# A decoder block's sub-norm: sum of squares from squared halves of the partitions, with one matmul of ones per head

## The chip, the cores and the metric

The kernel runs on one core of a Trainium2 chip. Its time is the device time of one execution in microseconds (us); the time of a kernel is the median over its runs. A core has five engines that run side by side, each through its own list of instructions in order: TensorE (PE in the profile, with its weight loads as PEld), VectorE (DVE), ScalarE (ACT), GpSimd (POOL) and SyncE (SP), which here only issues DMA transfers. GpSimd issues transfers too, those that add to what lies in SBUF.

## The reference, cut to what matters

One decoder block over 512 tokens of width 1024, all in float32:

```
h = rmsnorm(x, norm_attn_g);  q, k, v, u_pool, u_gate = split(h @ w_in)
for each of 8 heads:                          # two query/key pairs of width 64, one value of width 128
    w = softmax(q1 k1) - lam * softmax(q2 k2) # causal
    o = rmsnorm(w @ v, subln_g) * (1 - lam_init)     # the sub-norm: over the head's 128 value dims
x = x + (sigmoid(g_A) * o + sigmoid(g_P) * pool) @ w_out
x = x + square(relu(rmsnorm(x, norm_mlp_g) @ w_up)) @ w_down
return rmsnorm(x, final_norm_g)
```

The sub-norm divides each head's output, for each token, by the root of the mean of its 128 squares.

## The kernel before, in words

Everything lies in SBUF as 128 partitions by free columns. Activations are mostly kept transposed, features on the partitions and the 512 tokens along the columns; so a head's output o is a 128 x 512 tile whose 128 partitions are the value dims, and the sub-norm's sum runs over the partitions. For that, TensorE multiplies with a matrix of ones (`onesr`), which leaves the sum on every partition.

All matmuls run on float32 data split in two: a rounded high part (fp32r) and the rest as a low part, so a product of two matrices is three matmuls, high by high, low by high, high by low. In the names a leading `wh_`/`wl_` is the high and low part of a weight, `wr_` the raw weight as a transfer brings it. ScalarE's cast makes the high part (L112), VectorE's subtract the low one (L113). For squares the same is done: `sqh` is ScalarE's square rounded to fp32r, `sql` the rest, and `ss` is the sum of ones by `sqh` and ones by `sql`, two matmuls into one bank (L430, L431). GpSimd makes `sql` from o times o (L427) minus `sqh` (L428); for the last head VectorE does. `rsqrt` then makes y = 1/root from `ss`, on ScalarE (L202 to L204) and VectorE.

The stages in the profiled execution, by their time:

- 0 to 60 us: row norm, transposes, the value projection v.
- 60 to 305 us: the heads, one after another. `attn` makes the scores s (L395, L396), the softmax (L397 to L408, tile p), the transposes t (L410) and wt, then o (L418) and the sub-norm. Between the heads' matmuls stand the projections k, q, gate and pool of the next heads as fillers, so that TensorE has work while ScalarE and VectorE do softmax.
- 288 to 348 us: the out projection. po (L582 to L584) adds up `wh_o`/`wl_o` by vh/vl for four row tiles of 128 tokens and two column halves of 512: first the four tiles of the first half, then those of the second. When a tile's second half is done, VectorE adds it to x (L588, `x<-po`), ScalarE squares it with a sum over its row (L562), makes the root (L572 to L574), VectorE refines it (L575, L576) and scales the row (L637, `h<-x`); TensorE transposes h, four 128 x 128 pieces for each of two halves (L645, h2T), and ScalarE (L657) and VectorE (L658) split that into `gab`.
- 349 to 672 us: the MLP, in a scheme of Strassen's kind with sums of weight blocks. Products um (L782 to L788) from `gab` and from sums `gss` (L603, L604, by way of `hw`), z, then dm (L875 to L878). The sums of weights come about by transfers that GpSimd issues (L686, `wga_`, `wal_`) and that add to what lies in SBUF.

The order of each engine's instructions isn't written by hand. A scheduler lays them out when the kernel is built, with its own simulated timeline, over all five engines, from the data dependencies and the buffers of the tile pools (a tag with `bufs=2` has two buffers; the raw weights `wr_` have two, so a new transfer waits until the older one's cast and split have read it). Any edit can therefore change the order in places far from it.

Of the kernel before, what the change touches and what calls it, by code (L numbers as in the profile page):

```python
# [12 lines left out]
F32R = mybir.dt.float32r  # L13
I32 = mybir.dt.int32
AF = mybir.ActivationFunctionType
ALU = mybir.AluOpType
# [6 lines left out]
H = 8  # L23
# [28 lines left out]
def block_kernel(ctx, tc, xT, x_tok, gains, pos, consts, w_in, w_v, w_pool, w_out, w_up, w_dn, out):  # L52
    nc = tc.nc
    V, A, G, T = nc.vector, nc.scalar, nc.gpsimd, nc.tensor
# [32 lines left out]
    def tmp(tag, name, shape=(P, S), dt=F32, bufs=2):  # L87
        return tp.tile(list(shape), dt, tag=tag, name=name, bufs=bufs)

    def f(ap):  # L90
        return ap.bitcast(F32)
# [50 lines left out]
    for i in range(2):  # L142
# [14 lines left out]
    onesr = cp.tile([P, P], F32R, name="onesr")  # L157
# [7 lines left out]
        out=mask[:, 384:512], in_=mask[:, 384:512], pattern=[[-1, P]],  # L165
# [34 lines left out]
    def rsqrt(dst, src, t, n):  # L200

        A.activation(out=dst, in_=src, func=AF.Ln, scale=1.0 / n, bias=eps)  # L202
        A.activation(out=dst, in_=dst, func=AF.Exp, scale=-0.5)
        A.activation(out=t, in_=dst, func=AF.Square, scale=1.0 / math.sqrt(n))  # L204
        V.scalar_tensor_tensor(out=t, in0=src, scalar=n * EPS, in1=t, op0=ALU.add, op1=ALU.mult)
        V.scalar_tensor_tensor(out=dst, in0=t, scalar=-3.0, in1=dst, op0=ALU.add, op1=ALU.mult)
# [10 lines left out]
    for n in range(2):  # L217
# [43 lines left out]
        for t in range(NT):  # L261
# [4 lines left out]
                out=vd[2], in0=av, scalar=rcol[:, t, 0:1], in1=vd[1],  # L266
# [26 lines left out]
        out=r_, in0=posf.rearrange("p (t o) -> p t o", o=1).to_broadcast(sh),  # L293
        in1=invc.rearrange("p (o f) -> p o f", o=1).to_broadcast(sh), op=ALU.mult,
# [68 lines left out]
    lo_, hi_ = slice(0, 64), slice(64, 128)  # L363
# [22 lines left out]
    def attn(h, qs, ks, kz):  # L386
        wt = wt_all
        for i in range(NT):
            N = (i + 1) * P
            qsl = slice(i * P, i * P + P)  # L390
            pr = tmp(f"p{i}", f"p{h}_{i}", (P, 2, N), bufs=1)
            st = tmp("st", f"st{h}_{i}", (P, 6), bufs=3)
            for c in range(2):
                s_ = sbk(f"s{h}_{i}_{c}")
                T.matmul(s_[:, :N], lhsT=qs[:, c, qsl], rhs=ks[:, c, :N], start=True, stop=False)  # L395
                T.matmul(s_[:, :N], lhsT=qs[:, c, qsl], rhs=kz[:, c, :N], start=False, stop=True)  # L396
                V.tensor_tensor_reduce(  # L397
                    out=pr[:, c, :N], in0=s_[:, :N], in1=mask[:, S - N :], scale=-0.125, scalar=-NEG,
                    op0=ALU.add, op1=ALU.min, accum_out=st[:, c : c + 1],
                )  # L400
                A.activation(out=pr[:, c, :N], in_=pr[:, c, :N], func=AF.Exp, scale=-1.0,  # L401
                             bias=st[:, c : c + 1], accum_out=st[:, 2 + c : 3 + c])
            V.reciprocal(out=st[:, 4:6], in_=st[:, 2:4])
            V.tensor_scalar(out=st[:, 5:6], in0=st[:, 5:6], scalar1=lvec, scalar2=None, op0=ALU.mult)
            A.activation(out=pr[:, 1, :N], in_=pr[:, 1, :N], func=AF.Copy, scale=st[:, 5:6])
            V.scalar_tensor_tensor(out=pr[:, 0, :N], in0=pr[:, 0, :N], scalar=st[:, 4:5], in1=pr[:, 1, :N],
                                   op0=ALU.mult, op1=ALU.add)
            t_ = tbk(f"t{h}_{i}")  # L408
            for j in range(i + 1):
                T.transpose(out=t_[:, j * P : j * P + P], in_=pr[:, 0, j * P : j * P + P], identity=ident)  # L410
            tv = t_[:, :N].rearrange("p (j q) -> p j q", q=P)
            A.copy(out=wt[:, 0, : i + 1, qsl], in_=tv)
            V.tensor_tensor(out=wt[:, 1, : i + 1, qsl], in0=tv, in1=f(wt)[:, 0, : i + 1, qsl], op=ALU.subtract)
        o_ = obk(f"o{h}")
        n = 0
        for vv, ww in ((vh, 0), (vl, 0), (vh, 1)):
            for j in range(NT):
                T.matmul(o_[:, j * P :], lhsT=vv[:, h, j * P : j * P + P], rhs=wt[:, ww, j, j * P :], start=n == 0, stop=n == 11,  # L418
                         skip_group_check=True)
                n += 1  # L420
        o = tmp("o", f"o{h}", bufs=2)
        A.copy(out=o, in_=o_)
        sqh = tmp("sqh", f"sqh{h}", dt=F32R, bufs=1)
        A.activation(out=sqh, in_=o_, func=AF.Square)
        sql = tmp("y", f"sql{h}", dt=F32R, bufs=1)
        sq = tmp("sq", f"sqo{h}")
        (V if h == H - 1 else G).tensor_tensor(out=sq, in0=o, in1=o, op=ALU.mult)  # L427
        (V if h == H - 1 else G).tensor_tensor(out=sql, in0=sq, in1=f(sqh), op=ALU.subtract)  # L428
        ss = obk(f"ss{h}")
        T.matmul(ss, lhsT=onesr, rhs=sqh, start=True, stop=False)  # L430
        T.matmul(ss, lhsT=onesr, rhs=sql, start=False, stop=True)  # L431
        y = tmp("y", f"y{h}", bufs=1)
        rsqrt(y, ss, sq, P)
        if h == H - 1:
            return o, y
        V.scalar_tensor_tensor(out=o, in0=o, scalar=subc, in1=y, op0=ALU.mult, op1=ALU.mult)
        return o, None
# [78 lines left out]
    for h in range(H):  # L516
        outs[h] = attn(h, *cur)
        cur = qk(h + 1) if h < H - 1 else None
        while nf < LAG[h]:
            fillers[nf]()  # L520
            nf += 1
            if nf % 5 == 0:
                g = nf // 5 - 1
                gt = state["gt", g]
                for i in range(2):
                    merge(2 * g + i, state["sg", g], outs[2 * g + i], gt[:, 2 * i], gt[:, 2 * i + 1], *state["p", g])
# [505 lines left out]
```

## Time and profile before

| what | value |
|---|---|
| median of 3 runs | 674.77 us (674.47 to 674.83) |
| the profiled execution | 674.09 us, its span 671.9 us |
| granted TensorE clock | 0.996 |
| TensorE busy | 663.1 us, 99% of the span, 3688 matmuls |
| VectorE, ScalarE, GpSimd busy | 526.1, 461.0, 112.0 us |
| DMA | 109.34 MB, mean 163 GB/s |

A row of a timeline begins with the start in us from the span's start and the length, then engine, line, operation, output<-input by the program's names, and in brackets how long the engine had idled before it and what ended that. Matmuls overlap in a pipeline, so their cost is read from one start to the next. The profiled execution is 0.68 us under the median of the runs.

### The profile page before, as it was taken

The numbers are of one execution on the slowest core, as the hardware profiler recorded it, in microseconds if no ns is written. First come the engines' busy times: TensorE is split into PE (matmuls) and PEld (weight loads), VectorE is DVE, ScalarE is ACT, GpSimd is POOL, SyncE is SP. The second block draws the span as 40 slices with busy tenths as digits, with TensorE's granted clock in tenths as the row PEclk, the third lists the DMA queues.
The fourth block names the chain that finished last, engine by engine and source line by source line (L and its number), as shares of the span: only waits on it lengthen the run. The fifth ranks groups of instructions, "written<-read, shape, count | busy, mean of one in ns | idle before, by whom it ended". The sixth has DMA issues, their size and how long they took to land.

```text
span 671.9 us, 9994 instructions
## 1 busy us (share of the span) xinstructions
PE 663.1 (99%) x3688; PEld 579.6 (86%) x3688; DVE 526.1 (78%) x882; ACT 461.0 (69%) x741; POOL 112.0 (17%) x130
## 2 busy tenths in 40 slices
PE   9999999999999999999999999999999999999995
PEld 7888888888888888888889988999889998899884
DVE  6855977799979986875588998657994599747995
ACT  8465587978887698884477975367743695256974
POOL 2001110142133212520202020202102021210120
PEclk9999999999999999999999999999999999999998
DMA  9416464435263365574976596776959578494863
GB/s 317 162 57 185 126 151 126 103 94 126 87 142 103 98 166 105 126 184 172 312 208 112 159 235 186 167 191 146 236 199 187 193 164 261 117 212 132 214 126 125
DMA packets 32880, 109.34 MB, mean 163 GB/s; under 512 B 4032, under 2 KB 4928, under 8 KB 32832
## 3 DMA queue, kind: packets, MB, share of 16 engines
q0 software_dynamic: 10656, 38.80, 32.3%
q1 hardware_dynamic: 21744, 69.38, 29.3%
q8 instruction: 29, 0.48, 0.3%
q10 hardware_dynamic: 432, 0.52, 0.2%
q14 instruction: 19, 0.16, 0.1%
HBM read 106.59 MB, written 2.10 MB: 162 GB/s over the span
## 4 chain that ended last, share of the span: by engine, by line
PE 98%; DMA 1%; DVE 0%; ACT 0%; issue 0%; SPq 0%
PE um L785 8%; PE um L788 8%; PE um L782 8%; PE dm L875 8%; PE dm L877 8%; PE dm L878 8%; PE v L235 2%; PE o L418 2%; PE ga L132 2%; PE ga L131 2%; PE gp L135 2%; PE gp L132 2%; PE k L132 2%; PE k L131 2%; PE gp L131 2%; PE k L135 2%
## 5 line engine op out<-in xcount | busy, mean ns | idle before, releaser
L877 PE MATMUL dm<-wh_dt,z 128*128 128x512 f32 (+1 forms) x128 | 49.5, 386 | 0.0
L878 PE MATMUL dm<-wl_dt,z 128*128 128x512 f32 (+1 forms) x128 | 49.4, 386 | 0.0
L875 PE MATMUL dm<-wh_dt,z 128*128 128x512 f32 (+1 forms) x128 | 49.0, 387 | 0.0
L785 PE MATMUL um<-gss,wh_ut 128*128 128x256 f32 x192 | 48.2, 283 | 0.0
L782 PE MATMUL um<-gss,wh_ut 128*128 128x256 f32 x192 | 48.0, 283 | 0.0
L401 ACT ACTIVATE p<-p,st 128x128 f32<-128x128 f32 (+3 forms) x64 | 35.7, 558 | 14.1 <-DVE st L397 13.8
L895 DVE TENSOR_TENSOR x<-x,dm 128x512 f32<-128x512 f32 x48 | 32.5, 681 | 16.3 <-PE dm L878 16.3
L112 ACT CAST wh_ut<-wga_uNone 128x1024 fp32r<-128x1024 f32 x24 | 24.9, 1050 | 29.7 <-PE dm L877 19.2
L112 ACT CAST wh_ub<-wr_u 128x1024 fp32r<-128x1024 f32 x24 | 25.1, 1050 | 22.1 <-PE um L785 9.8
L686 POOL DMA_DIRECT2D wga_dNone<-w_dn x16 | 14.2, 885 | 154.2 <-DVE wl_dt L113 154.2
L113 DVE TENSOR_TENSOR wl_ut<-wga_uNone,wh_ut 128x1024 fp32r<-128x1024 f32 x24 | 29.1, 1221 | 13.0 <-ACT wh_ut L112 12.9
L877 PE MATMUL dm<-wh_db,z 128*128 128x512 f32 x96 | 37.2, 389 | 0.0
L878 PE MATMUL dm<-wl_db,z 128*128 128x512 f32 x96 | 37.2, 389 | 0.0
L785 PEld LDWEIGHTS um<-gss,wh_ut 128*128 128x128 f32 x192 | 36.9, 192 | 0.0
L782 PEld LDWEIGHTS um<-gss,wh_ut 128*128 128x128 f32 x192 | 36.8, 192 | 0.0
L875 PE MATMUL dm<-wh_db,z 128*128 128x512 f32 x96 | 35.7, 389 | 0.0
L113 DVE TENSOR_TENSOR wl_ub<-wr_u,wh_ub 128x1024 fp32r<-128x1024 f32 x24 | 29.1, 1219 | 7.4 <-ACT wh_ub L112 7.4
L686 POOL DMA_DIRECT2D wga_uNone<-w_up x18 | 15.6, 865 | 115.8 <-DVE wl_ut L113 81.4
L112 ACT CAST wh_dt<-wga_dNone 128x1024 fp32r<-128x1024 f32 x24 | 24.9, 1049 | 14.4 <-issue 6.7
L755 DVE TENSOR_TENSOR z<-rawz,z 128x1024 fp32r<-128x1024 f32 x28 | 33.6, 1218 | 0.5 <-ACT z L752 0.5
L397 DVE CUSTOM_DVE_ANT_0 p<-s,mask 128x128 f32<-128x128 f32 (+3 forms) x64 | 30.3, 484 | 3.6 <-PE s L396 3.5
L785 PE MATMUL um<-gab,wh_ub 128*128 128x256 f32 x128 | 32.5, 283 | 0.0
(324 smaller groups left out, 2203.3 us busy)
## 6 DMA issues: line engine op xcount, KB each, us to landing
wr_u<-w_up SPq DMA_DIRECT2D x24, 512.0 KB, 5.4
wr_d<-w_dn SPq DMA_DIRECT2D x24, 512.0 KB, 4.2
wga_uNone<-w_up POOLq DMA_DIRECT2D x18, 512.0 KB, 7.2
wga_dNone<-w_dn POOLq DMA_DIRECT2D x16, 512.0 KB, 5.7
wr_k<-w_in SPq DMA_DIRECT2D x8, 512.0 KB, 3.3
wr_ga<-w_in SPq DMA_DIRECT2D x8, 512.0 KB, 3.3
wr_gp<-w_in SPq DMA_DIRECT2D x8, 512.0 KB, 4.2
wl_ga<-w_in POOLq DMA_DIRECT2D x8, 512.0 KB, 5.4
```

The costliest lines, as they stand in the source:

```text
L112: ins = A.copy(out=hi[:, sl], in_=raw[:, sl])
L113: (eng or G).tensor_tensor(out=lo[:, sl], in0=raw[:, sl], in1=f(hi)[:, sl], op=ALU.subtract)
L131: T.matmul(acc, lhsT=hi[:, c], rhs=rh[:, k, :], start=k == 0, stop=False)
L132: T.matmul(acc, lhsT=hi[:, c], rhs=rl[k], start=False, stop=False)
L401: A.activation(out=pr[:, c, :N], in_=pr[:, c, :N], func=AF.Exp, scale=-1.0, bias=st[:, c : c + 1], accum_out=st[:, 2 + c : 3 + c])
L755: lo = V.tensor_tensor(out=z[:, 1], in0=r, in1=f(z[:, 0]), op=ALU.subtract)
L782: m = T.matmul(a_, lhsT=hi[:, c], rhs=rh[:, k, :], start=p + k == 0 and onto is None, stop=False, skip_group_check=True)
L785: T.matmul(a_, lhsT=hi[:, c], rhs=rl[:, k, :], start=False, stop=False, skip_group_check=True)
L788: m = T.matmul(a_, lhsT=lo[:, c], rhs=rh[:, k, :], start=False, stop=k == 3, skip_group_check=True)
L875: m = T.matmul(a_, lhsT=zh, rhs=hi[:, sl], start=p == 0 and start, stop=False, skip_group_check=True)
L877: T.matmul(a_, lhsT=zl, rhs=hi[:, sl], start=False, stop=False, skip_group_check=True)
L878: end = T.matmul(a_, lhsT=zh, rhs=lo[:, sl], start=False, stop=p == 3, skip_group_check=True)
```

## The change

The sum over 128 partitions is split into a sum of two halves and one sum over the partitions. ScalarE squares the lower 64 partitions (`lo_`) and the upper 64 (`hi_`) apart, both into partitions 0 to 63. GpSimd (VectorE for the last head) adds them. ScalarE's copy makes the rounded high part in the lower half of the new tile `parts`, and GpSimd's subtract puts the low part into its upper half. One matmul of ones over all 128 partitions of `parts` then gives the sum. After L428 the changed kernel's line numbers are one higher.

```diff
         A.copy(out=o, in_=o_)
-        sqh = tmp("sqh", f"sqh{h}", dt=F32R, bufs=1)
-        A.activation(out=sqh, in_=o_, func=AF.Square)
-        sql = tmp("y", f"sql{h}", dt=F32R, bufs=1)
         sq = tmp("sq", f"sqo{h}")
-        (V if h == H - 1 else G).tensor_tensor(out=sq, in0=o, in1=o, op=ALU.mult)
-        (V if h == H - 1 else G).tensor_tensor(out=sql, in0=sq, in1=f(sqh), op=ALU.subtract)
+        upper = tmp("y", f"squ{h}", bufs=1)
+        A.activation(out=sq[lo_], in_=o_[lo_], func=AF.Square)
+        A.activation(out=upper[lo_], in_=o_[hi_], func=AF.Square)
+        (V if h == H - 1 else G).tensor_tensor(out=sq[lo_], in0=sq[lo_], in1=upper[lo_], op=ALU.add)
+        parts = tmp("sqh", f"sqp{h}", dt=F32R, bufs=1)
+        A.copy(out=parts[lo_], in_=sq[lo_])
+        (V if h == H - 1 else G).tensor_tensor(out=parts[hi_], in0=sq[lo_], in1=f(parts)[lo_], op=ALU.subtract)
         ss = obk(f"ss{h}")
-        T.matmul(ss, lhsT=onesr, rhs=sqh, start=True, stop=False)
-        T.matmul(ss, lhsT=onesr, rhs=sql, start=False, stop=True)
+        T.matmul(ss, lhsT=onesr, rhs=parts, start=True, stop=True)
```

The scheduler writes other orders with it. In the rows below a number behind a name only tells tiles apart; `x4` is four like rows in a run.

On ScalarE at the end of the out projection, where the row norm of tiles 0 and 1 begins, there stands before:

```order
L112 CAST wh_o_3_3164<-wr_o_3_3162 128x1024
L562 ACTIVATE rawz,st_2995<-x_2986 128x512 x4
L112 CAST wh_ub_0_0_3391<-wr_u_0_0_3375 128x1024
L562 ACTIVATE rawz,st_2995<-x_2986 128x512
L572 ACTIVATE st_2995<-st_2995 128x1
L573 ACTIVATE st_2995<-st_2995 128x1
L562 ACTIVATE rawz,st_2995<-x_2986 128x512
L574 ACTIVATE st_2995<-st_2995 128x1
L572 ACTIVATE st_2995<-st_2995 128x1
L112 CAST wh_ub_0_1_3395<-wr_u_0_1_3376 128x1024
```

and now:

```order
L112 CAST wh_ub_0_0_3399<-wr_u_0_0_3383 128x1024
L559 ACTIVATE rawz<-rawz 128x1024
L112 CAST wh_o_3_3172<-wr_o_3_3170 128x1024
L563 ACTIVATE rawz,st_3003<-x_2994 128x512 x4
L112 CAST wh_ub_0_1_3403<-wr_u_0_1_3384 128x1024
L563 ACTIVATE rawz,st_3003<-x_2994 128x512
L573 ACTIVATE st_3003<-st_3003 128x1
L574 ACTIVATE st_3003<-st_3003 128x1
L575 ACTIVATE st_3003<-st_3003 128x1
L563 ACTIVATE rawz,st_3003<-x_2994 128x512
```

The cast of `wh_ub_0_1` has moved from behind the second halves' squares of tiles 0 and 1 to ahead of both; the cast of `wh_ub_0_0` has moved ahead of that of `wh_o_3`.

On VectorE at the same place, from the second-half sum of tile 0 on, there stands before:

```order
L588 TENSOR_TENSOR x_2986<-po_0_3168,x_2986 128x512
L588 TENSOR_TENSOR x_2986<-po_1_3217,x_2986 128x512
L575 SCALAR_TENSOR_TENSOR st_2995<-st_2995 128x1
L576 SCALAR_TENSOR_TENSOR st_2995<-st_2995 128x1
L637 SCALAR_TENSOR_TENSOR h_2988<-x_2986,st_2995,rawz 128x1024
L113 TENSOR_TENSOR wl_ub_0_1_3396<-wr_u_0_1_3376,wh_ub_0_1_3395 128x1024
L575 SCALAR_TENSOR_TENSOR st_2995<-st_2995 128x1
L576 SCALAR_TENSOR_TENSOR st_2995<-st_2995 128x1
L637 SCALAR_TENSOR_TENSOR h_2988<-x_2986,st_2995,rawz 128x1024
L588 TENSOR_TENSOR x_2986<-po_2_3266,x_2986 128x512
```

and now:

```order
L589 TENSOR_TENSOR x_2994<-po_0_3176,x_2994 128x512
L113 TENSOR_TENSOR wl_ub_0_1_3404<-wr_u_0_1_3384,wh_ub_0_1_3403 128x1024
L589 TENSOR_TENSOR x_2994<-po_1_3225,x_2994 128x512
L576 SCALAR_TENSOR_TENSOR st_3003<-st_3003 128x1
L577 SCALAR_TENSOR_TENSOR st_3003<-st_3003 128x1
L638 SCALAR_TENSOR_TENSOR h_2996<-x_2994,st_3003,rawz 128x1024
L576 SCALAR_TENSOR_TENSOR st_3003<-st_3003 128x1
L577 SCALAR_TENSOR_TENSOR st_3003<-st_3003 128x1
L638 SCALAR_TENSOR_TENSOR h_2996<-x_2994,st_3003,rawz 128x1024
L589 TENSOR_TENSOR x_2994<-po_2_3274,x_2994 128x512
```

The split `wl_ub_0_1` has moved ahead of the sum of tile 1 and of the scaling of tile 0. Further on, a second such split (`wl_ub_0_1` of the next block, which stood ahead of the first `gab`) now stands behind h of tile 2, and `x<-po_3` behind it, with one row of `hw` between that and h of tile 3; before, `x<-po_3` stood ahead of h of tile 2.

On TensorE, the transposes of tiles 0 and 1 within the last tile's po, before:

```order
L645 MATMUL h2T_0_3201<-ident,h_2988 128x128 x4
L645 MATMUL h2T_1_3206<-ident,h_2988 128x128 x4
L582 MATMUL po_3_3318<-wh_o_2_3158,vh 128x512
L583 MATMUL po_3_3318<-wl_o_2_3159,vh 128x512
L584 MATMUL po_3_3318<-wh_o_2_3158,vl 128x512
L582 MATMUL po_3_3318<-wh_o_2_3158,vh 128x512
L583 MATMUL po_3_3318<-wl_o_2_3159,vh 128x512
L645 MATMUL h2T_0_3250<-ident,h_2988 128x128 x4
L645 MATMUL h2T_1_3255<-ident,h_2988 128x128 x4
```

and now:

```order
L584 MATMUL po_3_3326<-wl_o_1_3161,vh 128x512
L646 MATMUL h2T_0_3209<-ident,h_2996 128x128 x4
L646 MATMUL h2T_1_3214<-ident,h_2996 128x128 x4
L646 MATMUL h2T_0_3258<-ident,h_2996 128x128 x4
L646 MATMUL h2T_1_3263<-ident,h_2996 128x128 x4
L585 MATMUL po_3_3326<-wh_o_1_3160,vl 128x512
```

The transposes of tile 1 have moved up to directly behind those of tile 0, and tile 0's stand one po matmul earlier. On SyncE the transfer of `wr_u_0_0` has moved ahead of those of `rawz`, both `wal_u` and one `wga_u`.

## The prediction

> **What bounds the kernel now.** I read the page's busy shares and its chain first, then the attention stage and the stage from the out projection to the MLP as stretches of time, then the rows in them.
>
> ```profile
> span 671.9 us, 9994 instructions
> PE 663.1 (99%) x3688; PEld 579.6 (86%) x3688; DVE 526.1 (78%) x882; ACT 461.0 (69%) x741; POOL 112.0 (17%) x130
> PE 98%; DMA 1%; DVE 0%; ACT 0%; issue 0%; SPq 0%
> ...
> 118.00:305.00 187.00, 186.94 (x911) 156.53 (x910) 157.99 (x358) 154.27 (x288) 55.25 (x52) 1.00 0.50 125
> ...
> 320.00:345.00 25.00, 25.00 (x115) 20.75 (x114) 14.61 (x27) 12.38 (x28) 3.48 (x4) 1.00 0.99 293
> ```
>
> TensorE is busy for 99% of the span and is 98% of the chain that ended last. The last two rows are stretches of the span (length, then busy time of PE, weight loads, DVE, ACT, POOL, granted clock, DMA share, GB/s). In both, attention (118 to 305) and the end of the out projection (320 to 345), PE never idles. So each matmul taken away is worth its pitch, as long as nothing that PE needs comes later than before. In the second stretch the DMA engines are 0.99 busy; there the schedule is tight.
>
> **What the change takes away.** Eight matmuls of 512 columns, one per head.
>
> ```profile
> 127.80 0.45 PE L430 MATMUL ss<-sqh,onesr 128*128 128x512 f32 x1
> 128.09 0.23 PE L396 MATMUL s<-kz,qs 128*128 128x128 f32 x1
> ...
> 130.04 0.39 PE L431 MATMUL ss<-sql,onesr 128*128 128x512 f32 x1
> 130.27 0.39 PE L132 MATMUL k<-xlb,wh_k 128*128 128x512 f32 x1
> ...
> L430 PE MATMUL ss<-sqh,onesr x8: 392/395/482, 127.8 to 309.8; 128*128 128x512 f32 x8
> L431 PE MATMUL ss<-sql,onesr x8: 388/388/478, 130.0 to 312.2; 128*128 128x512 f32 x8
> ```
>
> The durations of 0.39 overlap; what counts is from one start to the next: 0.23 us (130.04 to 130.27) and 0.29 (127.80 to 128.09). Eight of them are 1.8 to 2.3 us; I take 1.8, since nearly all rows of this width stand at 0.23.
>
> **What it adds.** Per head one copy (L422) stays, one square over 128 partitions becomes two over 64, and a third ScalarE row, the copy of the sum into `parts`, is new. GpSimd keeps two rows, now of 64 partitions.
>
> ```profile
> L422 ACT COPY o<-o x8: 569/586/587, 123.9 to 304.5; 128x512 f32<-128x512 f32 x8
> L424 ACT ACTIVATE sqh<-o x8: 588/604/606, 124.4 to 305.0; 128x512 fp32r<-128x512 f32 x8
> L382 ACT CAST ks<-kz 64x512 fp32r<-64x512 f32 x16 | 9.9, 620 | 0.4
> L427 POOL TENSOR_TENSOR sqo<-o x7: 1035/1041/1736, 124.6 to 290.6; 128x512 f32<-128x512 f32 x7
> L428 POOL TENSOR_TENSOR sql<-sqo,sqh x7: 1293/1357/2158, 125.7 to 291.8; 128x512 fp32r<-128x512 f32 x7
> ```
>
> A ScalarE row of 512 columns costs 0.59 to 0.62 whether it has 64 partitions (L382) or 128 (L424), so sixteen more are at most 16 x 0.62 = 9.9 us of ScalarE, which has 187.0 - 154.3 = 32.7 free in the attention stage: hidden, unless one stands ahead of something that PE wants at once. The copy into `parts` is such a place: it makes ScalarE wait for GpSimd's add, and behind it in ScalarE's queue stand the softmax rows (L401, L405, L412) that PE's transposes need. GpSimd's two rows keep their number; how long they take on 64 partitions no row shows, so I bound them from above by the rows of 128 (1.04 to 1.74 and 1.29 to 2.16) and from below by half of these; the longest decides here. The sum of squares comes later: o's copy and the two squares 1.8, the add 1.7, the copy 0.6, the subtract 2.2, at worst 6.3 us. In the new order the remaining `ss` matmul stands behind at least 7 us of other PE rows after the last matmul of o, so PE isn't held by it. Cost taken: 0; bounds 0 to 0.5 us a head, 0 to 4 in all.
>
> **What it moves.** The scheduler wrote the order of every engine anew, and the place that matters is 328 to 372 us: end of out projection, row norm of the four row tiles (x, then h), transposes h2T, first MLP products um.
>
> ```profile
> 328.87 1.23 DVE L113 TENSOR_TENSOR wl_o<-wr_o,wh_o 128x1024 fp32r<-128x1024 f32 x1 [0.19 <-ACT wh_o L112]
> ...
> 336.04 0.63 ACT L562 ACTIVATE rawz<-x 128x512 f32<-128x512 f32 x1 [3.81 <-DVE x L588]
> ...
> 337.24 0.62 ACT L562 ACTIVATE rawz<-x 128x512 f32<-128x512 f32 x1
> ...
> 338.31 1.06 ACT L112 CAST wh_ub<-wr_u 128x1024 fp32r<-128x1024 f32 x1
> ...
> 338.52 1.28 DVE L637 SCALAR_TENSOR_TENSOR h<-x,st,rawz 128x1024 f32<-128x1024 f32 x1
> 339.72 1.22 DVE L113 TENSOR_TENSOR wl_ub<-wr_u,wh_ub 128x1024 fp32r<-128x1024 f32 x1
> ...
> 341.30 1.28 DVE L637 SCALAR_TENSOR_TENSOR h<-x,st,rawz 128x1024 f32<-128x1024 f32 x1
> 342.50 0.68 DVE L588 TENSOR_TENSOR x<-po,x 128x512 f32<-128x512 f32 x1
> ...
> q0 software_dynamic: 372, 1.39, 79.5%
> q1 hardware_dynamic: 223, 0.79, 23.7%
> ...
> wr_u<-w_up SPq DMA_DIRECT2D x1, 512.0 KB, 8.2
> ...
> wr_o<-w_out SPq DMA_DIRECT2D x1, 512.0 KB, 3.3
> ```
>
> Before, ScalarE squares tiles 0 and 1 (336.04, 337.24) and only then casts wh_ub_0_1 (338.31). Now that cast stands ahead of both squares, and on VectorE the split wl_ub_0_1 ahead of x<-po_1 and h of tile 0. The cast needs the transfer of wr_u_0_1. Its buffer comes free when wl_o_3 ends (328.87 + 1.23 = 330.1), and it takes 8.2 us, so it lands at 338.3, just when the cast starts. It's slow since from 330 to 339 the 16 DMA engines are 79.5% taken by GpSimd's accumulating transfers (q0) and 23.7% by SyncE's (q1). An equal transfer at 317.3, alone, took 3.3. The new order keeps what frees the buffer, so I take 338.3 again (bounds 333.4 and 338.3). So tile 0's square, which could start at 336, now starts behind the cast, at 339.3; from square to h it was 338.52 - 336.04 = 2.5, so h of tile 0 goes from 341.6 to 342.9, h of tile 1 (x<-po_1 is queued behind wl_ub) to about 344.6.
>
> The Trainium skill, DMA: Bandwidth & Descriptors, section "Queues, rings and completion order", has each DMA engine go round between its queue rows packet by packet, which the two rows for q0 and q1 bear out. The same page's section "Anatomy of one DMA — SWDGE (gpsimd) path" fits 2.0 us plus bytes over 436e3; an estimate by it for 512 KB is 3.2 us, which the 3.3 us bears out and the 8.2 doesn't; with it the transfer would land at 333.3, the sum would be -0.9.
>
> When PE wants them, and what follows:
>
> ```profile
> 344.36 0.49 PE L645 MATMUL h2T<-ident,h 128*128 128x128 f32 x3
> ...
> 346.38 0.38 PE L645 MATMUL h2T<-ident,h 128*128 128x128 f32 x2
> ...
> 348.86 0.28 PE L782 MATMUL um<-gab,wh_ub 128*128 128x256 f32 x1
> ...
> 367.90 0.28 PE L782 MATMUL um<-gss,wh_ut 128*128 128x256 f32 x1
> ...
> 346.98 1.88 DVE L658 TENSOR_TENSOR gab<-h2T,gab 128x512 fp32r<-128x512 f32 x3
> ...
> 349.50 0.68 DVE L588 TENSOR_TENSOR x<-po,x 128x512 f32<-128x512 f32 x1
> ...
> 352.23 1.29 DVE L637 SCALAR_TENSOR_TENSOR h<-x,st,rawz 128x1024 f32<-128x1024 f32 x1
> 353.43 2.35 DVE L113 TENSOR_TENSOR wl_ut<-wga_uNone,wh_ut 128x1024 fp32r<-128x1024 f32 x2
> 355.70 0.68 DVE L651 TENSOR_TENSOR hw<-h2T,hw 128x512 f32<-128x512 f32 x1
> ...
> 363.58 1.05 ACT L112 CAST wh_ut<-wga_uNone 128x1024 fp32r<-128x1024 f32 x1 [1.68 <-DMA wga_uNone<-w_up]
> ...
> 365.80 0.68 DVE L604 TENSOR_TENSOR gss<-hw,gss 128x512 fp32r<-128x512 f32 x1
> ```
>
> 1. Tile 1's transposes stood at 346.38. Eight sums fewer, one po product fewer ahead and the five between the two tiles' transposes now behind: 346.38 - 14 x 0.227 = 343.2. h of tile 1 ends at 344.6: PE idles 1.4 us.
> 2. um stood at 348.86, so 347.0 now. But x<-po_2 (0.7), its square, cast and split (2.9) and two or three gab (1.2 to 1.9) are queued from 344.6 on: gab is whole at about 350. PE is then 3 us behind its own rows (the 1.4 is in it).
> 3. VectorE goes on: from 348.2 four gab 2.5 (1.88 for three at 346.98), two narrow rows 0.4, h of tile 2 1.2, a split of wl_ub that stood earlier 1.2, then x<-po_3 at about 353.4, which was at 349.50. From x to h it was 2.7 (349.50 to 352.23), with one hw row of 0.6 now between: h of tile 3 at 356.7, 4.5 late.
> 4. wl_ut behind it (353.43) is 4.5 late too. It frees the buffer for GpSimd's next accumulating transfer, for which ScalarE's cast already waited (363.58, 1.68 idle), and behind that stands the last gss of the second sum, over at 366.48, now 371.0. PE wants it at 367.90 - 1.8 = 366.1: in all 4.9 us of idle PE, which contains the 3.
>
> Behind that, PE bounds again and nothing gives the time back. **Sum:** -1.8 + 4.9 = +3.1. The profiled execution took 674.09: 677.2. The median of the runs is 674.77, 0.68 above it, so I say 677.9 for the median.
>
> **The rivals.** The transfer decides, and the sum goes with its landing L: net = +3.1 + (L - 338.3), down to a floor. The floor: even with no hold, the split of wl_ub and the hw row ahead of h of tile 3 leave gss some 0.9 us late, -1.8 + 0.9 = -0.9.
>
> *The transfer lands between 333.4 and 336.5* (3.3 to 6.4 us after 330.1). Net -0.9 to +1.3, 673.9 to 676.1 in the median. For it: wr_u_0_0 goes ahead of four other transfers in SyncE's queue, so GpSimd's accumulations may start later and leave it room. Against it: they are the same bytes, and the row of 8.2. The fit of the Trainium skill, DMA: Bandwidth & Descriptors, would put the transfer at the lower end, 673.9; the 8.2 us of the trace speaks against it.
>
> *The full saving.* L is under 334.3 and the 0.9 is hidden too: -1.8 to -2.3, so 672.5 to 673.0. For it: PE is the bound everywhere else. It needs a transfer 4 us faster and a free VectorE, which is 14.61 of 25 busy at 320 to 345, but in the wrong order.
>
> *ScalarE's new wait.* The copy into `parts` waits for GpSimd's add (up to 1.7 us) in front of softmax rows, and PE's transposes come late by 0.5 us in each of 7 heads: 3.5 beside the saving, +1.7 with a quiet transition, 676.5; with the main case 681. Against it: 32.7 us free on ScalarE.
>
> **How the numbers follow.** Under 0.2% (1.35 us) no difference can be told in this kernel. Main case (net +1.4 to +5, 676.2 to 680) 0.58; ScalarE's wait 0.08, also slower; the transfer in between 0.21, same; full saving 0.13, faster. The time is the main case's, 677.9. The range reaches down into the second case's lower end and leaves out the full saving: 673.3 to 680.6; main case alone 676.2 to 680.0.
>
> **What would show it.** PE's idle time at the transposes of tile 1 (about 1.4 us, released by h), at the first um (1.6 more, gab), at the second sum's um (about 2, gss): right. ScalarE's cast wh_ub_0_1 waiting for the transfer near 338 and tile 0's square behind it: the step itself; landing before 335 breaks it. Eight `ss` at 0.23: the saving. Idle PE ahead of transposes in 60 to 305: ScalarE's rival. A span under 670.5 would make the forecast wrong altogether.

## The result, and the profile after

| | before | changed | ratio |
|---|---|---|---|
| median | 674.62 us (673.77 to 674.87, 6 runs) | 678.65 us (677.77 to 680.44, 6 runs) | 1.0065 (95%: 1.0055 to 1.0076) |
| profiled execution | 674.09, span 671.9 | 678.69, span 676.9 | |

The change makes the kernel slower by 4.0 us, and the forecast was 677.9. The time came out near the forecast; the place did not. The page of the changed kernel (span, busy times, the chain that ended last) and what TensorE waited for (total, times, longest):

```profile
span 676.9 us, 9991 instructions
PE 663.8 (98%) x3680; PEld 579.8 (86%) x3680; DVE 526.0 (78%) x882; ACT 468.6 (69%) x757; POOL 111.0 (16%) x130
PE 77%; DVE 8%; ACT 6%; DMA 5%; issue 3%; SPq 0%; POOL 0%; ACTq 0%; DVEq 0%; POOLq 0%
...
PE s L395 <- ACT ks L382: 3.6, 1, 3.6
...
PE um L786 <- DVE gss L605: 0.5, 1, 0.5
PE t L410 <- DVE p L406: 0.4, 1, 0.4
PE um L783 <- ACT rawz L811: 0.4, 1, 0.4
```

TensorE was 98% of the chain and is now 77%. The chain leaves it in two stretches. The first, from 176.5 to 266.6 us, runs mostly over VectorE and ScalarE and ends in the one long wait, 3.6 us in attention. The second, from 318 to 378.6, holds the transition from out projection to MLP, where the forecast put 4.9 us; there are two waits of 0.5 and 0.4 in it. To see what each place costs, the same TensorE instruction (the n-th of its kind) is found in both traces; its start after minus its start before:

| place, start before | later by |
|---|---|
| projections, 9 to 116 us | -0.18 |
| attention, 261.5, ahead of head 7's scores | -1.42 |
| attention, 293.8 | +3.97 |
| um, 350.8 | +3.70 |
| first dm, 390.9, and from there to the end | +5.02 |

So the saved matmuls show (-1.2 by 261 us, with a stall of 0.4 in it), head 7's scores cost 5.4, and the transition 1.3. The stall and what follows it, TensorE's rows and two stretches (busy times in the order of the engines, then the granted clock):

```profile
262.62 0.41 PE L432 MATMUL ss<-sqp,onesr 128*128 128x512 f32 x1
266.60 0.33 PE L395 MATMUL s<-ks,qs 128*128 128x128 f32 x1 [3.57 <-ACT ks L382]
...
262.00:266.60 4.60, 1.03 (x6) 0.49 (x4) 4.37 (x10) 3.76 (x8) 0.48 (x1) 1.00 0.65 120
268.00:271.40 3.40, 3.40 (x11) 2.57 (x10) 0.38 (x2) 3.37 (x5) 0.88 (x1) 0.53 0.26 25
```

TensorE idles 3.57 us; and from 268.0 to 271.4 the clock granted is 0.53, which costs 3.4 x 0.47 = 1.6 us more. Together that is 5.2 of the 5.4. Why ks is late stands in the rows of the other engines, VectorE's rotation of head 7's k and GpSimd's two rows of the sub-norm, first before, then after:

```profile
258.73 0.68 DVE L353 TENSOR_TENSOR swk<-swk,tab 128x512 f32<-128x512 f32 x1
259.45 0.68 DVE L354 TENSOR_TENSOR q1k<-q1k,swk 128x512 f32<-128x512 f32 x1
...
254.69 1.03 POOL L427 TENSOR_TENSOR sqo<-o 128x512 f32<-128x512 f32 x1 [3.34 <-ACT o L422]
255.81 1.30 POOL L428 TENSOR_TENSOR sql<-sqo,sqh 128x512 fp32r<-128x512 f32 x1
```

```profile
259.44 1.42 DVE L353 TENSOR_TENSOR swk<-swk,tab 128x512 f32<-128x512 f32 x1
...
261.39 1.63 DVE L354 TENSOR_TENSOR q1k<-q1k,swk 128x512 f32<-128x512 f32 x1
...
259.01 1.30 POOL L427 TENSOR_TENSOR sqo<-sqo,squ 64x512 f32<-64x512 f32 x1 [6.62 <-ACT squ L426]
...
261.19 1.29 POOL L430 TENSOR_TENSOR sqp<-sqo,sqp 64x512 fp32r<-64x512 f32 x1
...
264.34 1.04 ACT L120 CAST wh_ga<-wr_ga 128x1024 fp32r<-128x1024 f32 x1
...
265.93 1.26 ACT L382 CAST ks<-kz 64x512 fp32r<-64x512 f32 x2
```

Before, GpSimd was done at 257.1, ahead of the two rotation rows. Now it starts only behind two squares, its subtract waits for ScalarE's copy besides, and both rows fall onto VectorE's: L353 takes 1.42 us beside GpSimd's add and L354 1.63 beside its subtract, where each took 0.68. Each of the two starts while GpSimd's row runs and ends 0.55 us behind that row's end. Together VectorE loses 1.7 us there. On top of that ScalarE's new order has a weight cast (1.04) and a softmax row ahead of ks. GpSimd's rows also aren't shorter for their 64 partitions: 1.30 and 1.29.

### The profile page after: what moved, and what is told of

The parts are those of the page before. It is cut to its first block, busy times and chain, and to the rows that moved or that the text cites. A ratio compares the mean times of both kernels' runs of the same rounds, so it can differ in the third digit from the quotient of the medians.

```text
span 676.9 us, 9991 instructions
## 1 busy us (share of the span) xinstructions
PE 663.8 (98%) x3680; PEld 579.8 (86%) x3680; DVE 526.0 (78%) x882; ACT 468.6 (69%) x757; POOL 111.0 (16%) x130
## 4 chain that ended last, share of the span: by engine, by line
PE 77%; DVE 8%; ACT 6%; DMA 5%; issue 3%; SPq 0%; POOL 0%; ACTq 0%; DVEq 0%; POOLq 0%
PE dm L878 7%; PE dm L876 7%; PE dm L879 7%; PE um L783 7%; PE um L789 7%; PE um L786 7%; DMA wga_uNone<-w_up 4%; PE v L235 2%; PE v L236 2%; PE v L237 2%; PE ga L131 2%; PE ga L132 2%; PE ga L135 2%; PE o L418 1%; PE k L132 1%
## 5 line engine op out<-in xcount | busy, mean ns | idle before, releaser
L786 PE MATMUL um<-gab,wh_ub 128*128 128x256 f32 x128 | 32.5, 283 | 0.0
L783 PE MATMUL um<-gab,wh_ub 128*128 128x256 f32 x128 | 32.5, 284 | 0.0
```

The lines of the kernel that those rows point to most:

```text
L783: m = T.matmul(a_, lhsT=hi[:, c], rhs=rh[:, k, :], start=p + k == 0 and onto is None, stop=False, skip_group_check=True)
L786: T.matmul(a_, lhsT=hi[:, c], rhs=rl[:, k, :], start=False, stop=False, skip_group_check=True)
```

## The experiments

Since any edit moves rows everywhere, most runs hold the order. At the end of the kernel body the instructions of each engine are chained, without waits, in an order given as a table of instruction numbers:

```diff
+    for row in ORDER:
+        last = None
+        for piece in row.split():
+            a, _, b = piece.partition("-")
+            for n in range(int(a), int(b or a) + 1):
+                this = nc.find_inst_by_name(f"I-{n}")
...
+                if last is not None:
+                    tc.add_manual_dep(this, last.name, mybir.DependencyInfo(mybir.DependencyClass.NoSync, ...
+                last = this
```

The table is the order of before or of the changed kernel, or a mixture. All times are medians, and the ratio is to runs of the kernel before on the same chip.

**1. The changed arithmetic in the order of before.** Edit: the table is that of before; only the sub-norm's rows are new.

> The changed arithmetic, with every engine's instructions held in the order of the kernel before (the second square directly behind the first, the copy into parts 0 to 4 ScalarE rows later, the one ss where the second ss stood). Theory A, the new order makes the loss and the arithmetic itself only saves eight matmul pitches: no idle TensorE in 60 to 372 us, 674.6 - 1.8 = 672.8 us (672.2 to 673.4). Rival B, the arithmetic itself costs (sixteen more ScalarE rows, ScalarE's wait for GpSimd's add): idle TensorE ahead of transposes or scores, 674.6 or more.

Measured: 679.27 us, ratio 1.0081 (1.0068 to 1.0094). Theory A fell: the order of before does not save the arithmetic. TensorE now waits at two other places, for p of head 4 and for ss of head 6. Rows of TensorE, VectorE and GpSimd of this kernel:

```profile
220.76 0.63 PE L410 MATMUL t<-ident,p 128*128 128x128 f32 x4 [1.93 <-DVE p L406]
...
301.34 0.50 PE L432 MATMUL ss<-sqp,onesr 128*128 128x512 f32 x1 [2.10 <-POOL sqp L430]
...
203.57 1.59 DVE L406 SCALAR_TENSOR_TENSOR p<-p,st 128x256 f32<-128x256 f32 x1
...
203.58 1.29 POOL L430 TENSOR_TENSOR sqp<-sqo,sqp 64x512 fp32r<-64x512 f32 x1 [2.17 <-ACT sqp L429]
...
297.29 2.01 POOL L427 TENSOR_TENSOR sqo<-sqo,squ 64x512 f32<-64x512 f32 x1 [6.42 <-ACT squ L426]
```

The p row of 256 columns takes 1.59 beside GpSimd's subtract; before, it stood alone and took 0.47. It isn't the p that TensorE waits for, but it sets VectorE back by 1.1 us, and VectorE is still that late when it comes to that p. And the chain square, add, copy, subtract ends 2.1 us after TensorE wants ss of head 6; its add, which starts beside a split on VectorE, takes 2.01. (The profiled execution of this kernel also lost 3.0 us at its very start, ahead of anything that was changed, where its matmuls stand 0.43 us apart up to about 11 us and those of before 0.23: 3.7 of its 6.8 us belong to attention.)

**2 and 3. Attention and transition apart.** Edit: the table of one kernel for attention, of the other for all instructions from the out projection on; first the order of before in attention and the changed kernel's behind it, then the other way round.

> As the first, but the instructions of the out projection and the MLP stand in the order of the changed kernel among themselves; attention stays in the order of before. The forecast's theory, the transition alone costs 4.9 us of idle TensorE: 677.7 us. Theory A, the loss is made by the stall at head 7's scores in attention, and the transition adds the 1.3 us seen in the changed kernel at most: 672.8 to 674.2 us. In between (the transition's chain hangs on a transfer that is itself released by earlier work and moves up with it): 674.2 to 675.

Measured: 681.97 us, 1.0114 (1.0100 to 1.0128). Both numbers missed, since attention in the order of before has stalls of its own with this arithmetic. What its trace tells is the step at the transition, read like the table above: +6.79 at the um, +7.79 at the first dm, so 1.0 us. It also shows the clock, a stretch behind the stall of 1.93 that this kernel has too (behind its stall of 2.10 at ss the clock was 0.50 once more, from 301.1 to 304.5):

```profile
219.00:223.00 4.00, 4.00 (x14) 3.20 (x12) 3.83 (x13) 3.88 (x9) 1.05 (x3) 0.57 0.65 180
```

> The changed kernel's own order in attention, the order of before among the instructions of the out projection and the MLP. Theory A: the stall at head 7's scores stays (3.6 us of idle TensorE and the slower matmuls behind it, 5.4 in all), the transition's 1.3 us go: 677.3 us (676.8 to 677.8). The forecast's theory (the transition makes the loss): 673 to 674 us.

Measured: 678.96 us, 1.0063 (1.0050 to 1.0076). The stall of 3.6 us at head 7's scores is there, and the transition costs nothing (+5.31 at the um, +5.32 at the first dm). The time is higher than the 677.3 expected: the clock stayed low longer behind the stall, from 266 to 273 us.

**4. Head 7's ks ahead on ScalarE.** Edit, in the changed kernel's table, on ScalarE:

```diff
 L380 CAST kz x2
+L382 CAST ks x2
 L120 CAST wh_ga
 L405 ACTIVATE p
-L382 CAST ks x2
 L401 ACTIVATE p
```

> The changed kernel in its own order but for one move on ScalarE: the two casts of ks of head 7 (L382) stand ahead of the weight cast of wh_ga and of one softmax row, not behind them. Theory A: the first ks is ready 1.6 us earlier, so the idle time of TensorE before head 7's scores goes from 3.6 to 2.0 us: 678.65 - 1.6 = 677.0 us. If the matmuls at half clock behind the stall come of its length and a stall of 2.0 us is too short for them, another 1.6 us go: 675.4. Rival: ScalarE's place does not matter, since the wait passes to GpSimd's or VectorE's half of ks: 678 or more.

Measured: 680.32 us, 1.0092 (1.0077 to 1.0107). The rival's number holds. The wait is shorter, and now VectorE ends it, though with a softmax row (L397) and not with its half of ks; a second wait follows, and behind them the clock is at half again (0.60 from 267 to 271):

```profile
265.52 0.33 PE L395 MATMUL s<-ks,qs 128*128 128x128 f32 x1 [1.98 <-DVE st L397]
...
267.01 0.51 PE L131 MATMUL u<-xh,wh_u 128*128 128x512 f32 x1 [1.05 <-DVE g L475]
```

ScalarE's order isn't the root. VectorE itself is late.

**5. GpSimd's rows cut to 64 columns, order of before.**

```diff
-        A.activation(out=sq[lo_], in_=o_[lo_], func=AF.Square)
+        A.activation(out=sq, in_=o_, func=AF.Square)
...
+        few = slice(0, S if h == H - 1 else 64)
-        (V if h == H - 1 else G).tensor_tensor(out=sq[lo_], in0=sq[lo_], in1=upper[lo_], op=ALU.add)
+        (V if h == H - 1 else G).tensor_tensor(out=sq[lo_, few], in0=sq[lo_, few], in1=upper[lo_, few], op=ALU.add)
-        A.copy(out=parts[lo_], in_=sq[lo_])
+        A.copy(out=parts, in_=sq)
...
```

> As e1_order_before (the changed arithmetic in the order of before), with GpSimd's add and subtract of heads 0 to 6 cut to 64 of 512 columns, so the sum lacks most of the upper squares and low parts; ScalarE's rows keep their number and length. Theory C, GpSimd's rows now lie beside VectorE's softmax and rotation rows and stretch them (in e1 the p row of 0.47 took 1.59 us): the idle time of 1.9 us at 220 and 2.1 us at 301 goes, TensorE waits for nothing in attention, 672.8 us (672.3 to 673.5). Rival D, the sixteen more ScalarE rows and ScalarE's wait make the delay: the waits stay within a few tenths, 677 us or more.

Measured: 672.81 us, 0.9983 (0.9974 to 0.9992). Theory C holds and D falls: with all of ScalarE's rows and its wait in place, the waits for p and ss shrink from 1.9 and 2.1 us to 0.26 and 0.31. The cut also shortens the chain to ss, so this run doesn't tell the sharing with VectorE from the chain's length; experiment 10 looks at that.

```profile
215.83 0.63 PE L410 MATMUL t<-ident,p 128*128 128x128 f32 x4 [0.26 <-DVE p L406]
294.12 0.50 PE L433 MATMUL ss<-sqp,onesr 128*128 128x512 f32 x1 [0.31 <-POOL sqp L431]
```

**6. The eight matmuls alone.** Edit: before, in its own order, without the low part of the squares.

```diff
-        sql = tmp("y", f"sql{h}", dt=F32R, bufs=1)
...
-        T.matmul(ss, lhsT=onesr, rhs=sqh, start=True, stop=False)
-        T.matmul(ss, lhsT=onesr, rhs=sql, start=False, stop=True)
+        T.matmul(ss, lhsT=onesr, rhs=sqh, start=True, stop=True)
```

> The kernel before in its own order, with the low part of the squares left out: no GpSimd rows in the sub-norm, one ss matmul per head where the second stood, ScalarE as before. This prices the eight matmuls alone: 674.3 - 1.8 = 672.5 us (672.0 to 672.9) if TensorE waits for nothing. If taking GpSimd's rows away from VectorE were worth something by itself, less than 672; if something else than the arithmetic makes kernels with one ss slow, over 674.

Measured: 672.07 us, 0.9966 (0.9954 to 0.9979). In its trace TensorE waits for nothing behind the start, and from 9 us on it gains 0.34 + 1.75 = 2.1 us, eight times 0.26. It's the fastest kernel of this study, and beats both, but it computes something less: the sum of the squares' high parts.

**7 and 8. VectorE in GpSimd's place.** The edit, once with the other rows in the order of before and once with no order held:

```diff
-        (V if h == H - 1 else G).tensor_tensor(out=sq[lo_], in0=sq[lo_], in1=upper[lo_], op=ALU.add)
+        V.tensor_tensor(out=sq[lo_], in0=sq[lo_], in1=upper[lo_], op=ALU.add)
...
-        (V if h == H - 1 else G).tensor_tensor(out=parts[hi_], in0=sq[lo_], in1=f(parts)[lo_], op=ALU.subtract)
+        V.tensor_tensor(out=parts[hi_], in0=sq[lo_], in1=f(parts)[lo_], op=ALU.subtract)
```

> The changed arithmetic with VectorE in GpSimd's place for all heads, the rest in the order of before (the add, the copy into parts and the subtract fall where the scheduler puts them). Theory C: no sharing, but 1.4 us more on VectorE a head in the softmax chain: less idle TensorE than in e1, 673 to 675.5 us. Rival D: as e1 or slower, 677 to 680.

Measured: 679.26 us, 1.0070 (1.0057 to 1.0083). Expected was 673 to 675.5; rival D's number came, by another way. No row of the sub-norm lies beside VectorE's now, but add and subtract stand in VectorE's queue behind softmax and rotation rows, and TensorE waits for the end of the chain, longest at head 2:

```profile
178.22 0.47 PE L432 MATMUL ss<-sqp,onesr 128*128 128x512 f32 x1 [2.54 <-DVE sqp L430]
```

> The changed kernel with VectorE in GpSimd's place for all heads and no order held. The scheduler now counts the rows where they run: if its blindness for the sharing made the stall at head 7's scores, that stall goes, 672.8 to 675; if orders that the scheduler writes for one ss are bad for another reason, 677 or more.

Measured: 683.78 us, 1.0141 (1.0126 to 1.0157). It's the second bracket. The stall at head 7's scores is gone, as the first had it, but the new order has four others in the out projection and the transition, this the longest.

```profile
305.56 0.79 PE L584 MATMUL po<-wl_o,vh 128*128 128x512 f32 x1 [4.40 <-DMA wl_o<-w_out]
```

So what an order costs is a matter of each order; a kernel that is one edit away can have its stalls anywhere.

**9. The whole arithmetic, mended.** Edit, in experiment 1's table: ScalarE at head 3, TensorE at head 6 (14 rows, twelve of them gate products), ScalarE at head 6:

```diff
 L426 ACTIVATE squ
+L429 CAST sqp
 L405 ACTIVATE p
 L412 CAST wt
-L429 CAST sqp
...
-L432 MATMUL ss
 L410 MATMUL t x2
...
 L131 MATMUL gp
+L432 MATMUL ss
...
-L202 ACTIVATE y
 L412 CAST wt
+L202 ACTIVATE y
 L203 ACTIVATE y
```

> The whole changed arithmetic, in the order of before as in e1, with three moves: head 3's copy into parts stands directly behind the squares (ScalarE idled 2 us there in e1), so that GpSimd's subtract ends before VectorE's p row; head 6's ss stands 14 TensorE rows later, and ScalarE's Ln for it behind the next copy of wt. If the two stalls of e1 are GpSimd's rows over a VectorE row and the longer chain to ss, both go: 672.8 to 674.0 us, faster than before. If they only pass to the next row: 676 or more.

Measured: 674.52 us, 0.9999 (0.9991 to 1.0008), not the 672.8 to 674.0 expected. The wait at ss is gone. The one for p only went from 1.93 to 1.63. The p row of 256 columns is back at 0.47, but GpSimd's add, which had not been moved, stretches one rotation row to 1.72 (1.45 before), and the subtract now the next to 1.02 (0.71 before). And TensorE, with the sums of four heads cut, comes 0.8 us earlier to a place where VectorE had just been in time:

```profile
217.37 0.41 PE L410 MATMUL t<-ident,p 128*128 128x128 f32 x2 [1.63 <-DVE p L406]
...
197.63 1.72 DVE L353 TENSOR_TENSOR swq<-swq,tab 128x512 f32<-128x512 f32 x1
...
200.36 1.02 DVE L354 TENSOR_TENSOR q1q<-q1q,swq 128x512 f32<-128x512 f32 x1
```

With the whole sum in two parts, no version here beat the kernel before.

**10. Sharing without the longer chain.**

```diff
+        if h < H - 1:
+            G.tensor_tensor(out=upper[hi_], in0=sq[hi_], in1=sq[hi_], op=ALU.add)
...
+        if h < H - 1:
+            G.tensor_tensor(out=upper[hi_], in0=sq[hi_], in1=sq[hi_], op=ALU.subtract)
```

> e5 (add and subtract over 64 columns, so the sum is incomplete and its chain is short) with a second GpSimd row of full length, 64 partitions by 512, behind each of the two, whose output nobody reads. The chain to ss stays short, and the full rows lie beside VectorE's again. If sharing with VectorE made the stall at 220, it comes back, with little wait at ss: 674.5 to 676.5 us. If the length of the chain made e1 slow: 672.8 to 673.3.

Measured: 674.30 us, 0.9996 (0.9987 to 1.0005), 1.5 us above experiment 5, with a wait of 1.03 for p (0.26 there) and 0.24 for ss. That lies between the two brackets: the sharing by itself costs 0.8 us of waits and 1.5 in the median. It comes from two VectorE rows beside GpSimd's rows of head 2, a p row at 170.15 (1.18 us, 0.47 in experiment 5) and L354 at 173.34 (1.16, there 0.75). The two rows at 200 to 204 that were stretched in experiment 1, to 1.72 and 1.59, take 0.76 and 0.62 here, since they start ahead of the long rows here. So this run repeats only a part of experiment 1's sharing, and how the rest of that loss divides between sharing and the longer chain isn't shown. One link of the chain is plain, the 2.1 us at ss of head 6.

**11. The same cut in the changed kernel's own order.**

> The changed kernel in its own order with GpSimd's add and subtract of heads 0 to 6 cut to 64 of 512 columns (an incomplete sum). The two rotation rows for k of head 7 that took 1.42 (two) and 1.63 us beside GpSimd's rows need 0.7 each: idle time before head 7's scores 3.6 to 1.9 us, 678.65 - 1.7 = 677.0; 675.3 if the slow clock behind the stall goes with it. If GpSimd has no part in that stall: 678 or more.

Measured: 674.06 us, 0.9993 (0.9984 to 1.0002): 4.6 us less than the changed kernel, more than expected. The wait at head 7's scores goes from 3.57 to 1.03, and no slow stretch follows it (granted clock 1.00 from 264 to 268). It's more than expected since VectorE also comes to the rotation earlier (L350 at 256.49 and not 258.06): GpSimd's rows had stretched rotation rows of earlier heads too, one at 232.59 to 1.70 us. What is left of the wait hangs on ScalarE's ks, behind the weight cast.

```profile
263.98 0.33 PE L395 MATMUL s<-ks,qs 128*128 128x128 f32 x1 [1.03 <-ACT ks L382]
```

**12. The transition alone.** Edit: experiment 5 with the changed kernel's table from the out projection on.

> e5, which has no stall in attention (672.8 us), with the order of the changed kernel among the instructions of the out projection and the MLP: the forecast's term by itself. Forecast: 4.9 us of idle TensorE between 340 and 372, 677.7 us. If the transition costs what the changed kernel shows behind its stall in attention: 1.3, 674.1. If nothing: 672.8.

Measured: 674.00 us, 0.9997 (0.9988 to 1.0006), 1.2 us above experiment 5. The forecast's 4.9 falls; 1.3 was right, with no stall ahead of it to hide behind.

```profile
368.12 0.38 PE L787 MATMUL um<-gss,wh_ut 128*128 128x256 f32 x1 [0.36 <-DVE gss L606]
```

## Why the prediction was right in its time and wrong in its place

- **The saving, -1.8 (bounds -1.8 to -2.3).** Right. 2.1 us in the trace of experiment 6; its ratio allows 1.4 to 3.1.
- **What it adds, cost 0 (bounds 0 to 4).** This is the term that failed, beyond its bounds. Measured: 5.4 us at head 7's scores in the changed kernel, which is 4.6 us faster when GpSimd's rows are cut. It took GpSimd's rows to cost nothing because their number stays and GpSimd is idle most of the time, and asked only whether ss comes in time. It did not ask what lies beside them on VectorE once they start later. The trace of before had the answer: of the 32 rows of L353 and L354, the six that started while a GpSimd tensor row ran took 1.4 us in the mean, the other 26 took 0.69. The spread of GpSimd's own rows in the prediction, 1.04 to 1.74 us, was a sign of it: the row of 1.74 lay beside a split on VectorE. The lower bound for these rows was wrong as well, since half the partitions did not halve them (1.30 and 1.29). And it looked for the danger on ScalarE, where 32.7 free us in 187 covered the new rows; experiment 5 bears that out. The engine that came late was VectorE, though it had 29.0 free by the same measure: a sum of free time shows for neither whether a row is late.
- **The clock** was not in the sum at all: 1.6 of the 5.4 us, behind the stall. The trace of before has no stall after its start, so no row could show it.
- **The transition, +4.9.** It measured 1.0 to 1.3 (experiments 2 and 12, the changed kernel). The order was read rightly: the cast wh_ub_0_1 does wait for its transfer with the squares queued behind it. In the changed kernel:

```profile
338.74 1.05 ACT L112 CAST wh_ub<-wr_u 128x1024 fp32r<-128x1024 f32 x1 [1.88 <-DMA wr_u<-w_up]
...
371.58 0.69 DVE L605 TENSOR_TENSOR gss<-hw,gss 128x512 fp32r<-128x512 f32 x1
372.32 0.39 PE L786 MATMUL um<-gss,wh_ut 128*128 128x256 f32 x1 [0.45 <-DVE gss L605]
```

  The step that failed is "the new order keeps what frees the buffer". The split wl_ub_0_0 had moved ahead of wl_o_3, and the buffer that it frees is the one that is free first. In experiment 12, where no stall in attention makes TensorE late, that split ends at 328.4 and not 330.1; the transfer is issued then, takes 7.3 us and not 8.2, and lands at 335.7 instead of 338.3:

```profile
327.14 1.23 DVE L113 TENSOR_TENSOR wl_ub<-wr_u,wh_ub 128x1024 fp32r<-128x1024 f32 x1 [4.36 <-ACT wh_ub L112]
...
335.77 1.05 ACT L112 CAST wh_ub<-wr_u 128x1024 fp32r<-128x1024 f32 x1 [3.01 <-DMA wr_u<-w_up]
```

  By the forecast's own formula, net = +3.1 + (L - 338.3), that gives +0.5. The first dm of this run starts 0.8 later than before: TensorE came to the transition 0.4 ahead, not the 1.8 of the forecast, and lost 1.2. So the rival "the transfer lands between 333.4 and 336.5" is what the transition did.
- **The other rivals.** "ScalarE's new wait" had the right stage and the right sign at a chance of 0.08, and named 0.5 us in each of seven heads. What came was one long stall at one head, by VectorE. Its place was the rotation of k and not the transposes.
- **The sum.** -1.8 + 0 + 4.9 = 3.1 against -1.7 + 5.4 + 1.3 = 5.0 from trace to trace, and 4.0 in the medians (the profiled execution of before lies 0.5 under its median). Two terms were wrong by 5.4 and 3.6 in opposite directions. That the time was right is luck, not a merit of its reasons.

## What to carry to other kernels

A row that moves to another time is a changed row, even where its engine is idle and its length stays: look at what the engines that it can hold up do in the new place. When the profile shows the same row with two lengths, find what lay beside the long ones before calling anything free. And where a scheduler writes the order, a change in arithmetic is measured by holding the order first, else the edit and the new order can't be told apart.

## What the runs showed of the hardware that had not been expected

- GpSimd's tensor rows stretch VectorE's rows with two inputs in SBUF from 0.68 to as much as 1.78 us (L353, L354). L350, of the same size with one input in PSUM, stays at 0.68 beside them. The Trainium skill, GPSIMD Engine Reference, section "1. Specifications", has the two engines share their SBUF interfaces, with contention for VectorE instructions of two SBUF inputs; the rows agree.
- Which of the two waits is decided by who starts first. In all traces here, a row of L353 or L354 that started 0.06 us or more behind a GpSimd tensor row and met it ended 0.55 or 0.56 us behind that row's end. One that started ahead of GpSimd's row and met no other kept its 0.68, and GpSimd's row grew, in the changed kernel at 170 us to 1.61 from 1.28.
- A GpSimd row of 512 columns on 64 partitions takes as long as one on 128: 1.28 to 1.30 us undisturbed with two different inputs, in both, and 1.03 or 1.04 with one tensor as both inputs (128 partitions in the kernel before, 64 in experiment 10). Half the partitions save nothing. Cut to 64 columns the subtract at head 3 takes 0.32.
- A stall of TensorE costs more than its length, and not always the same. Behind 3.57 us the clock was 0.53 for 3.4 us in one execution and near 0.5 for 6.8 us in another kernel's; behind the same stall of 1.93 us it was 0.57 for 4 us in experiment 2 and stayed at 1.00 in experiment 1. Each slow stretch in these traces lasted 3.4 us (experiments 2, 4 and 7, the changed kernel) or twice that (experiments 3 and 8), and behind the stalls of 1.63 us and less in experiments 9 to 12 there was none. The runs of the changed kernel spread over 2.7 us, those of before over 1.1.
